# Seven block products in the last hidden group of the second block's MLP

## The chip, the cores and the metric

One NeuronCore of one Trainium2 chip runs the whole program. The metric is the device time in microseconds (us) of one execution; lower is better. A kernel's time is the median of its runs.

## The reference

Two transformer blocks work one after the other on 512 tokens of width 1024, all in float32. The change touches only the end of the second one, its MLP (y = hidden states, w1 is 1024 x 4096, w2 is 4096 x 1024):

```python
def _sq_relu_mlp(h, w1, w2):
    return jnp.square(jax.nn.relu(h @ w1)) @ w2

        y_x = _sq_relu_mlp(_modulate(x, g_pre_mlp[l], sh2, sc2), w_mlp_in[l], w_mlp_out[l])
        x = x + gt2 * _rmsnorm(y_x, g_post_mlp[l])
```

So: project up, square the ReLU, project down, normalise each token's 1024 values, scale by a gated gain, and add the residual.

## The kernel before

**Numbers.** Each float32 operand is split in a high part (rounded by ScalarE, L147) and a low part (the rest, by VectorE, L148), and a product is three matmuls: high by high, high by low, low by high (`mm3`, L150 to L154). All matmuls named below have a 128x128 stationary and a 128x512 moving operand.

**The MLP** (`mlp_seven`, called from `dense_two`, L1276). The 4096 hidden features are 32 tiles `j` of 128, in 4 groups of 8. For each group, `up(j)` makes eight tiles of the hidden activations (8 x 24 matmuls), and then the group is multiplied with its 1024 rows of w2 and added to the output.

**Groups 0 to 2** do the second part, `down(g)`, with seven block products in place of eight (Strassen's method in Winograd's form). Tokens and features are cut in two halves each. `operands` (L1298) builds four sums and differences of the quarter blocks of the hidden activations in a scratch tile (part of `gg`) and splits them; `less` (L1363) makes differences of the blocks of w2 on POOL, in place; `times` (L1343) multiplies one pair of blocks: two token tiles `tau`, two feature pairs `q`, two `i`, three matmuls, that is 24. The weights of a product are two tiles (`m2w<group><product><q>`), each loaded by one DMA of 512 KB in a ring of 6 buffers (`rb`), and split in a ring of 5 (`wh`, `wl`). Each product has two PSUM banks; its result goes to its own accumulator `Y[n]` in SBUF, by ScalarE in group 0 and by an add of VectorE afterwards (L1355, L1357).

**Then** `join()` (L1384) adds the seven accumulators up on POOL to four joined blocks, the quarters of the output: 14 adds of 128x512. The blocks are Y[2], Y[3] (token tiles 0 and 1, left and right half of the columns) and Y[4], Y[6] (token tiles 2 and 3).

**Group 3**, the last, is plain: `up` splits the activations as they are (L1330), and `token_major` (L790) multiplies them in two halves of 512 columns. A half is four token tiles x 8 `k` x 3 matmuls, so group 3 has 192 matmuls. In half 0 all four token tiles advance together, weight tile by weight tile; in half 1 (`in_turn`) one token tile is finished after the other. `evac` (L1412) adds the PSUM bank to the joined block (L1414), squares it with ScalarE for the norm (L1232), multiplies by the gain (L1416), and in half 1 POOL ends the norm (L1236, L1237), VectorE adds the residual (`post`, L1244, two halves) and SP stores it (L1419).

**Order.** The framework's scheduler lays the instructions of every engine out in one fixed order when the kernel is built: it takes what its own model of the times says is ready, the earliest in the program first. An engine then works strictly in that order, and a tile's buffer is handed on when its last reader is done. SP issues all weight loads, in order too.

Of the kernel before, what the change touches and what calls it, by code (L numbers as in the profile page):

```python
# [8 lines left out]
F32 = mybir.dt.float32  # L9
F32R = mybir.dt.float32r  # L10
# [99 lines left out]
RATIO = 1.6  # L110
TURN = "vavp"
# [18 lines left out]
class Build:  # L130
# [94 lines left out]
    def mod_T(self, x, cols_, quads, t, name, r=None):  # L225

        nc = self.nc
        xr = self.ep.tile([P, D], F32, tag="xr", name=name + "x", bufs=2)
# [5 lines left out]
        for qd in range(2):  # L234
            pt = self.turned(xr, qd, name)
            v = self.ep.tile([P, 4, P], F32, tag="v", name=f"{name}v{qd}", bufs=2)
# [991 lines left out]
    def squares(self, src, ss, half, name, tag="sqr"):  # L1228
# [3 lines left out]
        nc.scalar.activation(out=j, in_=src, func=AF.Square, accum_out=ss[:, half:half + 1])  # L1232
        if half == 0:
            nc.gpsimd.tensor_scalar(out=ss[:, 0:1], in0=ss[:, 0:1], scalar1=1.0 / D, scalar2=EPS, op0=ALU.mult, op1=ALU.add)
            return None
# [11 lines left out]
    def dense_two(self):  # L1247
# [26 lines left out]
        with ExitStack() as ph:  # L1274
            self.ep = ph.enter_context(tc.tile_pool(name="ep3", bufs=2, reuse_waits="tile"))
            self.mlp_seven(hT, a["w_mlp_in_2"][0], a["w_mlp_out_2"][0], y, gg, "m2")  # L1276

    def mlp_seven(self, hT, w1, w2, y, gg, name):

        nc = self.nc
        ac = nc.scalar.activation
        tt = nc.vector.tensor_tensor
        pt = nc.gpsimd.tensor_tensor
        ep = self.ep
        G = 8
        NG = NJ // G
        quads = [self.quad(f"{name}hid{i}").rearrange("p a b c -> p (a b c)") for i in range(2)]
        hid = quads + [ep.tile([P, 3584], F32R, tag=f"hid{i}", name=f"{name}hid{i + 2}", bufs=1) for i in range(2)]  # L1290
        more = ep.tile([P, 4, 512], F32, tag="more", name=name + "more", bufs=1)
        Y = {q: [y[i][:, h * 512:h * 512 + 512] for h in range(2)] for i, q in enumerate((2, 3, 4, 6))}
        Y[1] = [more[:, 0], more[:, 1]]
        Y[5] = [more[:, 2], more[:, 3]]
        Y[7] = [gg[:, 1, h * 512:h * 512 + 512] for h in range(2)]
        sums = gg[:, 0, :].rearrange("p (o t) -> p o t", o=4)

        def operands(g, p, st):  # L1298

            a11, a21, a12, a22 = st[:, 0, 0:256], st[:, 0, 256:512], st[:, 1, 0:256], st[:, 1, 256:512]  # L1300
            tt(out=sums[:, 0], in0=a21, in1=a22, op=ALU.add)
            tt(out=sums[:, 2], in0=a11, in1=a21, op=ALU.subtract)
            tt(out=sums[:, 1], in0=sums[:, 0], in1=a11, op=ALU.subtract)
            tt(out=sums[:, 3], in0=a12, in1=sums[:, 1], op=ALU.subtract)
            hi, lo = parts_of(p)
            self.split(hi[:, 3:7], lo[:, 3:7], sums)
            self.split(hi[:, 1:3].rearrange("p o t -> p (o t)"), lo[:, 1:3].rearrange("p o t -> p (o t)"), st[:, 1])

        def parts_of(p):
            return [hid[p][:, x * 1792:(x + 1) * 1792].rearrange("p (o t) -> p o t", o=7) for x in range(2)]  # L1310

        def plain(j):

            return hid[j % G // 2][:, j % 2 * 1024:j % 2 * 1024 + 1024].rearrange("p (x t) -> p x t", x=2)

        def up(j, st):
            wh, wl = self.weights(f"{name}u{j}", [(0, self.kview(w1, 0, KC, j * P, P))], KC, P, eng=nc.gpsimd if j < WPJ else None)
            acc = self.ps("s", f"{name}up{j}")
            nsp = 2 if j < NSP else 1
            w = SEQ // nsp  # L1320
            for sp in range(nsp):
                cols = slice(sp * w, (sp + 1) * w)
                for k in range(KC):
                    hqd = hT[k // 4]
                    self.mm3(acc[:, cols], wh[:, k, :], wl[:, k, :], hqd[:, k % 4, 0, cols], hqd[:, k % 4, 1, cols], k == 0, k == KC - 1)
            s = st[:, j % 2]
            ac(out=s, in_=acc, func=AF.Relu)
            nc.vector.scalar_tensor_tensor(out=s, in0=acc, scalar=0.0, in1=s, op0=ALU.max, op1=ALU.mult)  # L1328
            if j // G == NG - 1:
                self.split(plain(j)[:, 0], plain(j)[:, 1], s)  # L1330
            elif j % 2 == 0:
                hi, lo = parts_of(j % G // 2)
                self.split(hi[:, 0], lo[:, 0], s[:, 0:256])

        def block(g, q, r, c):

            t = ep.tile([P, 1024], F32, tag="rb", name=f"{name}d{g}{q}{r}{c}", bufs=6).rearrange("p (a b) -> p a b", a=2)
            j = g * G + 4 * q
            src = w2[j * P:(j + 4) * P, c * 512:c * 512 + 512].rearrange("(i r p) e -> r p i e", r=2, p=P)[r]
            nc.sync.dma_start(out=t, in_=src)  # L1340
            return t

        def times(g, n, o, b):  # L1343

# [14 lines left out]
        def down(g):  # L1359
            def blocks(r, c):  # L1360
                return [block(g, q, r, c) for q in range(2)]
# [89 lines left out]
```

## Time and profile before

| | us |
|---|---|
| median of 3 runs | 1255.91 (1252.36 to 1256.43) |
| the profiled execution, its own time | 1260.07 |
| its span, first to last instruction | 1258.3 |
| PE busy | 1213.5 (96%) |
| DVE busy | 844.6 (67%) |
| POOL busy | 355.1 (28%) |

PE is TensorE's matmuls, PEld its weight loads, DVE VectorE, ACT ScalarE, POOL GpSimd, SP SyncE (which issues DMAs). The span is 1.8 us shorter than the execution's own time. [...] A matmul's own duration (about 0.39 us) is longer than the distance from one start to the next, since they overlap; so costs of matmuls are taken from a stretch divided by their count.

### The profile page before, as it was taken

Reading aid. Unit: us, or ns where it says so; the run is one execution under the profiler, and the core shown is the slowest. Engines: PE = TensorE matmul, PEld = TensorE weight load, DVE = VectorE, ACT = ScalarE, POOL = GpSimd, SP = SyncE. Lnnn points to the kernel's source line nnn. Section 1 sums busy time; section 2 is a strip of 40 time slices with the busy share of each in tenths; the row PEclk is TensorE's granted clock in tenths of the full one; section 3 lists DMA queues with packets and bytes.
Section 4 is the critical chain, followed back from the end, with each engine's and each line's share of the span. In section 5 each row is a group of like instructions: output and inputs, shape, how many; then the busy total and the mean of one; then the engine's idle time right before and its main releaser. Section 6 shows DMA issues by size and latency. Waiting matters only on the chain. (4 is left out here: it accounts for less than half of the span.)

```text
span 1258.3 us, 16992 instructions
## 1 busy us (share of the span) xinstructions
PE 1213.5 (96%) x6316; PEld 1017.5 (81%) x6316; DVE 844.6 (67%) x1410; ACT 567.3 (45%) x1068; POOL 355.1 (28%) x370
## 2 busy tenths in 40 slices
PE   7899999999999999999999999999899999999997
PEld 6898888779888878888889878777798888888885
DVE  3799766597898854346355557574868678777744
ACT  5576656434223313225254546463546454343431
POOL 2787552252010000000014124030642504205502
PEclk9899999999999999999999999999999999999999
DMA  6222222365678734134145311215443643524421
GB/s 165 64 60 53 57 63 68 101 183 154 197 220 258 240 119 138 67 101 135 67 151 157 84 53 52 85 38 201 124 162 102 185 123 117 147 81 134 150 68 67
DMA packets 151707, 150.71 MB, mean 120 GB/s; under 512 B 14345, under 2 KB 115480, under 8 KB 151624
## 3 DMA queue, kind: packets, MB, share of 16 engines
q1 hardware_dynamic: 147224, 139.41, 36.4%
q0 software_dynamic: 4400, 10.22, 2.6%
q8 instruction: 49, 0.80, 0.3%
q14 instruction: 34, 0.28, 0.1%
HBM read 143.24 MB, written 6.36 MB: 119 GB/s over the span
## 5 line engine op out<-in xcount | busy, mean ns | idle before, releaser
L1365 POOL TENSOR_TENSOR m2d<-m2d,m2d 128x1024 f32<-128x1024 f32 x24 | 71.2, 2981 | 162.2 <-DVE m2w220l L148 51.5
L898 DVE SCALAR_TENSOR_TENSOR macc<-mod,silu_c,macc 128x1024 f32<-128x1024 f32 x56 | 76.1, 1369 | 15.5 <-DMA mod<-in_w_mod_dram 15.2
L975 DVE SCALAR_TENSOR_TENSOR xa<-m1d,r,xa 128x512 f32<-128x512 f32 x32 | 23.8, 746 | 37.5 <-PE m1d L154 37.5
L918 POOL DMA_DIRECT2D modrows<-mrow x8 | 3.9, 492 | 146.4 <-DVE mrow L916 91.9
L147 ACT ACTIVATE m2hid<-m2sq 128x512 fp32r<-128x512 f32 (+1 forms) x32 | 17.6, 551 | 49.1 <-DVE m2sq L1328 49.1
L147 ACT ACTIVATE m1hid<-m1sq 128x512 fp32r<-128x512 f32 x32 | 20.0, 630 | 38.3 <-DVE m1sq L844 38.3
L148 DVE TENSOR_TENSOR npl<-t,nph 128x512 fp32r<-128x512 f32 x32 | 21.7, 682 | 16.4 <-ACT nph L147 16.3
L194 POOL TENSOR_SCALAR p<-p,d 128x512 f32<-128x512 f32 x8 | 14.0, 1752 | 57.1 <-DVE d L1116 27.3
L148 DVE TENSOR_TENSOR m2hid<-m2sq,m2hid 128x512 fp32r<-128x512 f32 (+1 forms) x32 | 24.3, 760 | 6.0 <-ACT m2hid L147 5.8
L181 POOL TENSOR_SCALAR w<-w,g_attn 128x384 f32<-128x384 f32 x20 | 25.8, 1297 | 9.1 <-DMA w<-in_w_in_dram 6.7
L148 DVE TENSOR_TENSOR m1hid<-m1sq,m1hid 128x512 fp32r<-128x512 f32 x32 | 22.0, 687 | 9.1 <-ACT m1hid L147 9.1
L683 DVE TENSOR_REDUCE mb<-sb 128x1 f32<-128x128 f32 (+3 forms) x32 | 15.6, 487 | 16.5 <-PE sb L680 16.4
L1115 ACT ACTIVATE p<-s,m 128x512 f32<-128x512 f32 x32 | 22.0, 688 | 5.8 <-DVE m L1113 5.8
L1069 POOL TENSOR_TENSOR tb<-G,nam 128x256 f32<-128x256 f32 x24 | 17.8, 774 | 22.1 <-DVE m L1109 12.5
L685 ACT ACTIVATE pb<-sb,mb 128x128 f32<-128x128 f32 (+3 forms) x32 | 16.8, 525 | 16.0 <-DVE mb L683 15.7
L843 ACT ACTIVATE m1re<-m1up 128x512 f32<-128x512 f32 x32 | 18.6, 583 | 10.1 <-PE m1up L154 9.8
L204 POOL TENSOR_SCALAR nc_0ss<-nc_0ss 128x1 f32<-128x1 f32 x1 | 0.2, 187 | 80.5 <-ACT nc_0x L256 80.5
L152 PE MATMUL pj<-w_0h,xnT 128*128 128x384 f32 (+1 forms) x48 | 18.0, 376 | 4.9 <-ACT pjs L407 3.9
L147 ACT ACTIVATE nph<-t 128x512 fp32r<-128x512 f32 x32 | 19.0, 595 | 7.5 <-PE t L1126 7.2
L981 POOL DMA_DIRECT2D xspill<-xa x4 | 2.6, 655 | 70.0 <-DVE xa L975 69.9
L844 DVE SCALAR_TENSOR_TENSOR m1sq<-m1up,m1re 128x512 f32<-128x512 f32 x32 | 21.8, 683 | 0.1
L1328 DVE SCALAR_TENSOR_TENSOR m2sq<-m2up,m2sq 128x512 f32<-128x512 f32 x32 | 21.9, 684 | 0.0
(2017 smaller groups left out, 4679.7 us busy)
## 6 DMA issues: line engine op xcount, KB each, us to landing
mod<-in_w_mod_dram SPq DMA_DIRECT2D x48, 512.0 KB, 4.6
m2d<-in_w_mlp_out_dram SPq DMA_DIRECT2D x44, 512.0 KB, 3.7
m1u<-in_w_up_dram SPq DMA_DIRECT2D x32, 512.0 KB, 4.3
m1d<-in_w_down_dram SPq DMA_DIRECT2D x32, 512.0 KB, 3.6
m2u<-in_w_mlp_in_dram SPq DMA_DIRECT2D x32, 512.0 KB, 4.1
w<-in_w_in_dram SPq DMA_DIRECT2D x16, 512.0 KB, 4.2
w<-in_w_in_dram SPq DMA_DIRECT2D x48, 128.0 KB, 2.6
o1w<-in_w_out_dram SPq DMA_DIRECT2D x8, 512.0 KB, 3.8
```

Of the source, the lines that this page charges most:

```text
L147: self.nc.scalar.activation(out=hi, in_=src, func=AF.Copy)
L148: (eng or self.nc.vector).tensor_tensor(out=lo, in0=src, in1=hi.bitcast(F32), op=ALU.subtract)
L152: mm(out=out, lhsT=lh, rhs=rh, start=start, stop=False)
L181: eng.tensor_scalar(out=rv[:, i], in0=rv[:, i], scalar1=g, scalar2=None, op0=ALU.mult)
L843: ac(out=r, in_=acc, func=AF.Relu)
L844: nc.vector.scalar_tensor_tensor(out=s, in0=acc, scalar=0.0, in1=r, op0=ALU.max, op1=ALU.mult)
L898: nc.vector.scalar_tensor_tensor(out=accs[s], in0=rw, scalar=sc[:, s, k:k + 1], in1=accs[s], op0=ALU.mult, op1=ALU.add)
L975: nc.vector.scalar_tensor_tensor(out=x[t][:, cols], in0=acc, scalar=r2[:, t:t + 1], in1=x[t][:, cols], op0=ALU.mult, op1=ALU.add)
L1069: nc.gpsimd.tensor_tensor(out=tb[:, h, y], in0=G[:, h, ::-1, o:o + 32][:, :, ::-1], in1=nam[:, y, :].unsqueeze(1).to_broadcast([P, 8, 32]) ...
L1115: ac(out=pr, in_=s, func=AF.Exp, bias=m[:, 2:3], accum_out=den[:, 0:1])
L1328: nc.vector.scalar_tensor_tensor(out=s, in0=acc, scalar=0.0, in1=s, op0=ALU.max, op1=ALU.mult)
L1365: pt(out=o, in0=x, in1=z, op=ALU.subtract)
```

## The change

Group 3 takes seven block products too. For this the accumulators are arranged otherwise: product 1 goes to two of them, Y[6] and Y[2], in every group, so six accumulators do (`into`), and `joined` has ten POOL adds in place of fourteen. It leaves the four joined blocks in Y[2], Y[3], Y[4], Y[5]. `last_seven` runs products 1, 5, 6, 7, 4, 3, 2 on group 3, and adds each straight to the joined blocks that it belongs to, some of it on POOL. The last product, number 2, is done one token tile after the other (`in_turn`). Its two blocks of w2 are loaded a second time, since the first copy has been overwritten by `less`. The operands are now built in place in the activation tile, after the split of its raw second half.

The core of the diff (the removed code is in the listing above; `last_plain` is added but not called, `mod_T` gets an unused argument, `block`, `parts_of` and `less` are as before):

```diff
+        def up(j, seven):
...
+            hi, lo = parts_of(j % G // 2)
+            if j % 2 == 0:
+                self.split(hi[:, 0], lo[:, 0], s[:, 0:256])
+                return
+            self.split(hi[:, 1:3].rearrange("p o t -> p (o t)"), lo[:, 1:3].rearrange("p o t -> p (o t)"), s)
+            a11, a21, a12, a22 = st[:, 0, 0:256], st[:, 0, 256:512], st[:, 1, 0:256], st[:, 1, 256:512]
+            tt(out=a22, in0=a21, in1=a22, op=ALU.add)
+            tt(out=a21, in0=a11, in1=a21, op=ALU.subtract)
+            tt(out=a11, in0=a22, in1=a11, op=ALU.subtract)
+            tt(out=a12, in0=a12, in1=a11, op=ALU.subtract)
+            self.split(hi[:, 3:7], lo[:, 3:7], st.rearrange("p f (x t) -> p (f x) t", x=2))
...
+        def times(g, n, o, b, evac, in_turn=False):
+
+            accs = [self.ps("a", f"{name}p{g}{n}{tau}") for tau in range(2)]
+            w = [self.parts(f"{name}w{g}{n}{q}", b[q], 2, 512) for q in range(2)]
+            for q, tau in ([(0, 0), (1, 0), (0, 1), (1, 1)] if in_turn else [(0, 0), (0, 1), (1, 0), (1, 1)]):
...
+                if in_turn and q == 1:
+                    evac(tau, accs[tau])
+            if not in_turn:
+                for tau in range(2):
+                    evac(tau, accs[tau])
+
+        def down(g):
+            def into(*ns):
+                def evac(tau, acc):
+                    for n, first in ns:
+                        if g == 0 and first:
+                            ac(out=Y[n][tau], in_=acc, func=AF.Copy)
+                        else:
+                            tt(out=Y[n][tau], in0=acc, in1=Y[n][tau], op=ALU.add)
...
+            times(g, 1, 0, b11, into((6, True), (2, True)))
...
+        def joined():
+
+            for out, p, q, op in ((7, 6, 7, ALU.add), (4, 7, 4, ALU.subtract), (3, 3, 5, ALU.add), (3, 6, 3, ALU.add), (5, 7, 5, ALU.add)):
+                for tau in range(2):
+                    pt(out=Y[out][tau], in0=Y[p][tau], in1=Y[q][tau], op=op)
...
+        def last_seven(done, fetch_x):
+
+            g = NG - 1
+            f = [ep.tile([P, 2, 512], F32, tag="st", name=f"{name}f{i}", bufs=2) for i in range(2)]
+            u, c = Y[6], Y[7]
+            p1, p5 = [[x[:, 0], x[:, 1]] for x in f]
+
+            def evac1(tau, acc):
+                ac(out=p1[tau], in_=acc, func=AF.Copy)
+                pt(out=Y[2][tau], in0=Y[2][tau], in1=p1[tau], op=ALU.add)
+
+            def evac5(tau, acc):
+                ac(out=p5[tau], in_=acc, func=AF.Copy)
+                for n in (3, 5):
+                    pt(out=Y[n][tau], in0=Y[n][tau], in1=p5[tau], op=ALU.add)
+
+            def evac6(tau, acc):
+                tt(out=u[tau], in0=acc, in1=p1[tau], op=ALU.add)
+                pt(out=Y[3][tau], in0=Y[3][tau], in1=u[tau], op=ALU.add)
+
+            def evac7(tau, acc):
+                tt(out=c[tau], in0=acc, in1=u[tau], op=ALU.add)
+                tt(out=Y[5][tau], in0=Y[5][tau], in1=c[tau], op=ALU.add)
+                done(2 + tau, 1, True, Y[5][tau])
+                pt(out=Y[4][tau], in0=Y[4][tau], in1=c[tau], op=ALU.add)
+
+            def evac4(tau, acc):
+                tt(out=Y[4][tau], in0=Y[4][tau], in1=acc, op=ALU.subtract)
+                done(2 + tau, 0, False, Y[4][tau])
+
+            def evac3(tau, acc):
+                tt(out=Y[3][tau], in0=acc, in1=Y[3][tau], op=ALU.add)
+                done(tau, 1, True, Y[3][tau])
+
+            def evac2(tau, acc):
+                tt(out=Y[2][tau], in0=acc, in1=Y[2][tau], op=ALU.add)
+                done(tau, 0, False, Y[2][tau])
+            b11 = blocks(g, 0, 0)
+            times(g, 1, 0, b11, evac1)
+            t1 = blocks(g, 0, 1)
+            less(t1, t1, b11)
+            times(g, 5, S1, t1, evac5)
+            t2 = blocks(g, 1, 1)
+            less(t2, t2, t1)
+            times(g, 6, S2, t2, evac6)
+            b21 = blocks(g, 1, 0)
+            less(b21, t2, b21)
+            b22 = blocks(g, 1, 1)
+            b12 = blocks(g, 0, 1)
+            less(b12, b22, b12)
+            times(g, 7, S3, b12, evac7)
+            fetch_x((2, 3))
+            times(g, 4, A22, b21, evac4)
+            times(g, 3, S4, b22, evac3)
+            fetch_x((0, 1))
+            times(g, 2, A12, blocks(g, 1, 0), evac2, True)
...
+            self.row(gg[:, 1, :], 5)
...
+            def done(t, half, first, z):
+                r = self.squares(z, ss2[t], 0 if first else 1, f"sk{half}{t}", "sqr")
+                nc.vector.tensor_tensor(out=z, in0=z, in1=gg[:, 1, half * 512:half * 512 + 512], op=ALU.mult)
+                if not first:
+                    for _, c in self.post(x[t], [Y[((2, 3), (4, 5))[t // 2][i]][t % 2] for i in range(2)], r):
+                        nc.sync.dma_start(out=self.out[0, t * P:(t + 1) * P, c], in_=x[t][:, c])
```

## Rows read from the trace of the kernel before

**Rows 1.** The page's first lines: span, and PE's busy time.

```profile
span 1258.3 us, 16992 instructions
PE 1213.5 (96%) x6316; PEld 1017.5 (81%) x6316; DVE 844.6 (67%) x1410; ACT 567.3 (45%) x1068; POOL 355.1 (28%) x370
```

**Rows 2.** Windows: group 1's down part, group 3's up part and products, the tail.

```profile
core 0: us, PE busy (x) PEld busy (x) DVE busy (x) ACT busy (x) POOL busy (x), PEclk, DMA share, GB/s
...
1038.04:1076.84 38.80, 38.80 (x169) 31.62 (x168) 35.37 (x29) 14.59 (x15) 21.14 (x8) 1.00 0.40 131
...
1160.44:1205.23 44.79, 44.79 (x193) 36.05 (x192) 28.68 (x26) 18.18 (x25) 16.60 (x11) 1.00 0.43 135
1205.23:1249.50 44.27, 44.27 (x193) 35.92 (x191) 19.58 (x26) 10.29 (x20) 5.66 (x10) 1.00 0.15 54
1249.50:1258.30 8.80, 0.23 (x1) 0.00 (x0) 2.80 (x4) 0.72 (x2) 1.30 (x2) 0.81 0.24 92
```

**Rows 3.** Windows of one tile's instructions: `m2p` (group 0's products), `m2d` (group 3's).

```profile
954.43:993.24 38.81, 38.81 (x168) 31.44 (x167) 0.00 (x0) 6.54 (x12) 1.00 0.41 128
...
1205.23:1249.50 44.27, 44.27 (x192) 35.92 (x191) 9.54 (x11) 4.22 (x4) 0.00 (x0) 1.00 0.15 54
```

**Rows 4.** Timeline of DVE after group 1's last up: start, duration, what.

```profile
1039.16 1.23 DVE L148 TENSOR_TENSOR m2w160l<-m2d,m2w160h 128x1024 fp32r<-128x1024 f32 x1 [1.65 <-ACT m2w160h L147]
...
1042.18 1.23 DVE L148 TENSOR_TENSOR m2w161l<-m2d,m2w161h 128x1024 fp32r<-128x1024 f32 x1 [0.28 <-ACT m2w161h L147]
...
1044.26 0.68 DVE L148 TENSOR_TENSOR m2hid<-m2sq,m2hid 128x512 fp32r<-128x512 f32 x1
...
1046.59 1.22 DVE L148 TENSOR_TENSOR m2hid<-g_post,m2hid 128x1024 fp32r<-128x1024 f32 x1
1048.01 3.14 DVE L148 TENSOR_TENSOR m2w121l<-m2d,m2w121h 128x1024 fp32r<-128x1024 f32 x1 [0.20 <-ACT m2w121h L147]
```

**Rows 5.** Timeline of PE: its return to product 5 in group 1.

```profile
1050.33 0.39 PE L152 MATMUL m2p<-m2w151h,m2hid 128*128 128x512 f32 x1
```

**Rows 6.** Timeline of all engines around product 7's weights in group 2.

```profile
1143.11 2.40 POOL L1365 TENSOR_TENSOR m2d<-m2d,m2d 128x1024 f32<-128x1024 f32 x1 [5.82 <-DVE m2w230l L148]
...
1145.48 2.27 POOL L1389 TENSOR_TENSOR y<-m2more,y 128x512 f32<-128x512 f32 x1
...
1147.71 3.39 POOL L1365 TENSOR_TENSOR m2d<-m2d,m2d 128x1024 f32<-128x1024 f32 x1
...
1151.07 1.29 POOL L1389 TENSOR_TENSOR y<-m2more,y 128x512 f32<-128x512 f32 x1
1151.13 1.06 ACT L147 ACTIVATE m2w271h<-m2d 128x1024 fp32r<-128x1024 f32 x1 [4.52 <-POOL m2d L1365]
```

**Rows 7.** DMA issues: the blocks of w2; KB each, us to landing.

```profile
m2d<-in_w_mlp_out_dram SPq DMA_DIRECT2D x44, 512.0 KB, 3.7
```

**Rows 8.** Groups of DVE from 1205.23 us on: count, busy us, mean ns, idle before.

```profile
L1244 DVE SCALAR_TENSOR_TENSOR xc<-y,ss,xc 128x512 f32<-128x512 f32 x8 | 5.7, 749 | 3.2 <-POOL ss L1237 3.2
L1416 DVE TENSOR_TENSOR y<-y,g_post 128x512 f32<-128x512 f32 x8 | 5.5, 690 | 4.0 <-ACT sk L1232 3.6 <-issue 0.3
L1414 DVE TENSOR_TENSOR y<-m2d,y 128x512 f32<-128x512 f32 x8 | 5.4, 687 | 6.1 <-PE m2d L154 6.1
```

**Rows 9.** Timeline of the tail, from the last matmul on.

```profile
1249.34 0.39 PE L154 MATMUL m2d<-m2d13h,m2hid 128*128 128x512 f32 x1
1249.76 0.69 DVE L1414 TENSOR_TENSOR y<-m2d,y 128x512 f32<-128x512 f32 x1 [1.10 <-PE m2d L154]
1250.55 0.63 ACT L1232 ACTIVATE sk<-y 128x512 f32<-128x512 f32 x1 [4.83 <-DVE y L1414]
...
1251.37 0.75 POOL L1236 TENSOR_SCALAR ss<-ss 128x1 f32<-128x1 f32 x1 [4.16 <-ACT sk L1232]
1252.21 0.55 POOL L1237 TENSOR_TENSOR ss<-ss,nhalf 128x1 f32<-128x1 f32 x1
1252.79 1.42 DVE L1244 SCALAR_TENSOR_TENSOR xc<-y,ss,xc 128x512 f32<-128x512 f32 x2 [0.80 <-POOL ss L1237]
```

More of the change, by code (lines that the diff above doesn't have):

```diff
@@ L110 @@
 RATIO = 1.6
+MRAW = 4
+RB_2 = 6
 TURN = "vavp"
@@ L223, in split_T, with mod_T @@
             self.split(quads[qd][:, :, 0, cols], quads[qd][:, :, 1, cols], self.turned(x, qd, name))
-    def mod_T(self, x, cols_, quads, t, name, r=None):
+    def mod_T(self, x, cols_, quads, t, name, r=None, tiles=None):
         nc = self.nc
-        xr = self.ep.tile([P, D], F32, tag="xr", name=name + "x", bufs=2)
+        xr, vtag = tiles or (self.ep.tile([P, D], F32, tag="xr", name=name + "x", bufs=2), "v")
         if r is None:
@@ L235, in mod_T @@
             pt = self.turned(xr, qd, name)
-            v = self.ep.tile([P, 4, P], F32, tag="v", name=f"{name}v{qd}", bufs=2)
+            v = self.ep.tile([P, 4, P], F32, tag=vtag, name=f"{name}v{qd}", bufs=2 if vtag == "v" else MRAW)
             for j in range(4):
@@ L1230, in squares @@
+    def squares(self, src, ss, second, name, tag="sqr"):
         nc = self.nc
         j = self.ep.tile([P, 512], F32, tag=tag, name=name, bufs=2)
-        nc.scalar.activation(out=j, in_=src, func=AF.Square, accum_out=ss[:, half:half + 1])
-        if half == 0:
+        nc.scalar.activation(out=j, in_=src, func=AF.Square, accum_out=ss[:, second:second + 1])
+        if not second:
             nc.gpsimd.tensor_scalar(out=ss[:, 0:1], in0=ss[:, 0:1], scalar1=1.0 / D, scalar2=EPS, op0=ALU.mult, op1=ALU.add)
@@ new lines, in dense_two @@
+            hidx = self.ep.tile([P, 7168], F32R, tag="hidx", name="m2hidx", bufs=1)
+            more = self.ep.tile([P, D], F32, tag="more", name="m2more", bufs=1)
+            Y = {n: [b[:, h * 512:h * 512 + 512] for h in range(2)]
+                 for n, b in ((2, y[0]), (3, y[1]), (4, y[2]), (5, y[3]), (6, more), (7, gg[:, 0, :]))}
+            self.row(gg[:, 1, :], 5)
+            last_ups, last_plain, last_seven = self.mlp_seven(hT, a["w_mlp_in_2"][0], a["w_mlp_out_2"][0], hidx, Y, RB_2, lambda: None, "m2")
@@ new lines, in dense_two, with fetch_x @@
+            x = {}
+            ss2 = [self.small("ss", f"ss2{t}") for t in range(NT)]
+            def fetch_x(ts):
+                for t in ts:
+                    x[t] = self.ep.tile([P, D], F32, tag="rb", name=f"xc{t}", bufs=RB_2)
+                    nc.sync.dma_start(out=x[t], in_=self.xspill2[t * P:(t + 1) * P, :])
+            def done(t, half, first, z):
[3 more added lines that the diff above has]
+                    for _, c in self.post(x[t], [Y[((2, 3), (4, 5))[t // 2][i]][t % 2] for i in range(2)], r):
@@ L1419, in evac @@
                         nc.sync.dma_start(out=self.out[0, t * P:(t + 1) * P, c], in_=x[t][:, c])
-            j = (NG - 1) * G
-            self.token_major(f"{name}d{half}", G,
-                             lambda q: self.weights(f"{name}d{half}{q}", [(0, self.kview(w2, j + 2 * q, 2, half * 512, 512))], 2, 512),
-                             lambda i: plain(j + i), evac, half == 1)
+            last_ups(True, lambda j: None)
+            last_seven(done, fetch_x)
 _INS = ['x', 'attn_norm_g', 'w_in', 'b_forget', 'q_norm_a', 'k_norm_a', 'sink_logits', 'q_norm_b', 'k_norm_b', 'w_out',
```

216 lines of the change are left out of this document (91 added, 125 removed).

## The prediction

> **What bounds the kernel now.** I read the page first, then the stretches of the second MLP, then single engines in the last of them. PE is busy for 96% of the span [rows 1], which alone says little, because matmuls overlap. The stretches say more [rows 2]: in a down part (group 1), in group 3's up part and in group 3's products PE is busy for the whole of each (38.80 of 38.80, 44.79 of 44.79, 44.27 of 44.27 us) at a granted clock of 1.00. No wait of PE is left to remove there; only fewer matmuls shorten it. The other engines have room, DVE least: 35.37 of 38.80 us in a down part with POOL at 21.14, but 19.58 of 44.27 in group 3's products, where POOL does 5.66. So the change takes work from the full engine and gives some to the two that have room in just that stretch.
>
> The kernel ends with a chain of dependent small steps after the last matmul, 8.80 us [rows 2, 9].
>
> **What is removed.** Group 3's plain products are 2 halves x 4 token tiles x 8 k x 3 = 192 matmuls, in 44.27 us, 0.2306 each. A group of seven products is 7 x 24 = 168, in 38.80 us, 0.2310 each [rows 3]. The difference is 24 matmuls: 44.27 - 38.80 = 5.5 us off PE. Up parts and groups 0 to 2 keep their matmul counts.
>
> **What is added, engine by engine.** Let P be the end of the last up, 1205.23 us, where product 1 of group 3 will start. A product lasts 38.80 / 7 = 5.54 us, so the order 1, 5, 6, 7, 4, 3, 2 puts product 7 at P + 16.6, product 2 at P + 33.3, and the end of PE at P + 38.8.
>
> DVE between P and the end: ten weight tiles to split (products 6, 7, 4, 3, 2; those of 1 and 5 are done during the ups) x 1.22 = 12.2 [rows 4]; twelve adds from PSUM x 0.69 = 8.2, eight multiplies by the gain x 0.69 = 5.5, eight residual steps x 0.75 = 6.0 [rows 8]; and the last pair's operands, two ops of 0.68, one of 1.22 and four smaller ones, say 4. That is 35.9, of which 2.8 lie in the tail as before [rows 9]: 33 us in 38.8. It fits, if POOL lets it.
>
> POOL: ten adds (two, four, two and two for products 1, 5, 6, 7) x 1.29 and two `less` for product 7 x 2.40 = 17.7 us when undisturbed [rows 6], 29.5 at the disturbed 2.27 and 3.39. It fits as well. The other six `less` of the group come before P, `joined` is shorter than `join` by four adds, and both lie under the ups.
>
> ACT gets four copies of PSUM (0.63 each, as its square of the same size [rows 9]) and the ten splits at 1.06 [rows 6]: 13 us beside the eight squares. No cost. SP issues 14 block loads in place of eight weight loads, which are spread over the stage at 3.7 us to landing [rows 7]; the x tiles now come later, behind product 7's and 4's splits, and are wanted only after product 4, 11 us on. No cost. The early gain row on POOL's queue is one DMA issue in a stage that is not changed. No cost. Product 1's second accumulator adds two DVE adds of 0.69 per group: 1.4 us in a down part where DVE has 38.80 - 35.37 = 3.4 us left [rows 2]. No cost while that is left.
>
> **Three places where it can leak.**
>
> First, the operands. The raw second half is now split before the in-place sums, which puts one ACT step of 0.6 and one DVE step of 0.68 ahead of the last split, and two more DVE adds come near it. In group 1 that split ended at 1047.81 [rows 4], and PE came back to the matmuls that use it at 1050.33 [rows 5]: 2.5 us spare. 1.3 + 1.4 = 2.7 uses them up. If the split slides past 1048, POOL's `less` meets it, and it takes 3.14 in place of 1.22 [rows 4]. Bounds: nothing, if the scheduler fills in other matmuls as it did there, to 2 us in each of four groups, 8 in all. I take 0.2 per group, near the lower end, since the spare time about equals the delay and PE had no gap in these stretches: 0.8.
>
> Second, product 7's weights. Their blocks reuse the buffers of product 6's, which in group 1 were split 2.4 and 5.4 us after the last up ended at 1038.0 [rows 4]. So: P + 2.4 and P + 5.4, plus 3.7 to landing [rows 7] gives P + 6.1 and P + 9.1; `less` at up to 3.39, one after the other, ends at P + 9.5 and P + 12.9 at the latest; split by ACT and DVE (2.3, up to 4.2 disturbed) ends at P + 12 to 14 and P + 15 to 17. PE wants them at P + 16.6 and P + 19.4. Two to four us spare. Bounds: nothing to 10 (second rival). I take nothing: the forecast has POOL do these `less` as soon as they are ready, and it has done so out of the program's order before: an add of `join` (L1389) ran between two `less` of the group before it [rows 6].
>
> Third, the tail. The last token tile follows the one before by 12 matmuls, 2.8 us; in the kernel before it was 24, 5.5 us. The residual step of the first one comes 1252.79 - 1249.73 = 3.06 us after its last matmul [rows 9], so it wants DVE 0.3 us after the last tile's add does. If the fixed order has it first, the add waits 0.3 + 1.42 = 1.7 us; otherwise it waits for nothing. Bounds 0 and 1.7; I take 0.4, as the add is ready first.
>
> **The sum.** -5.5 + 0.8 + 0 + 0.4 = -4.3 us. It stands against the profiled execution, 1260.1 us (span 1258.3): 1255.8. The median of the runs shown is 4.2 lower, 1255.9, and I carry that difference over: **1251.6 us**. Its own bounds: with nothing lost 1250.4, with 2 us more lost 1253.6.
>
> **Rivals.** About 0.3% (3.8 us) is what a measurement of this kernel can tell from no change; below 1252.1 counts as faster.
>
> *DVE becomes the second bound, and the gain goes into its waits.* A split beside a POOL op took 3.14 in place of 1.22, 1.9 more [rows 4], and ten splits and twelve POOL ops now share 38.8 us. If half the splits meet one, DVE needs 33 + 5 x 1.9 = 42.5 us, 3.7 too many. Against it: in group 2 the second tile of product 7 waited 4.52 us for POOL and was split at 1151.13 + 1.06 + 1.22 = 1153.4 [rows 6], while PE wanted it at 1160.44 - 2.8 = 1157.7: 4.3 us of lead even so. For it: product 2's blocks are loaded late, into buffers that product 3's splits set free, so a late DVE delays that load too. Price: about 2.5 us more than the forecast, 1254.1. Chance 0.29.
>
> What POOL costs DVE could also follow a stricter rule. The row shows an op of 1.22 us stretched to 3.14 beside one of POOL's [rows 4]. If every POOL op held DVE up for its whole length, 33 + 17.7 = 50.7 us would be wanted of 38.8, and the kernel would be 11.9 - 5.5 + 0.4 = 6.8 us slower, 1262.7. [...] Chance 0.03.
>
> *POOL's order starves product 7 (slower).* POOL works strictly in its built order. In the program the adds of products 1 and 5 stand ahead of the `less` for product 7. If the scheduler leaves the second `less` behind them, it starts when product 5's four adds are done: they begin at P + 11.1 + 0.6, last 4 x 2.27, and end at P + 20.8; then 3.39 for the `less`, 1.06 and up to 3.14 for the split: P + 28.4, against P + 19.4 wanted. PE idles 9 us, and the rest follows it: -5.5 + 9 + 1.2 = +4.7, 1260.6. With both `less` behind them it is 3.4 more. It decides once product 7's second split ends later than P + 28, 9.3 us after PE wants it. For it: the two adds of product 1 alone use up the spare time. Against it: [rows 6], as above. Chance 0.10.
>
> *It doesn't do what it says.* The scheduler lays out the whole program anew, and other tiles share the space; the earlier stages could shift by a few us either way. Nothing in their program changes. Chance 0.02, 1256.
>
> **How the numbers follow.** The forecast has 0.56, the first rival 0.29, the lock 0.03, POOL's order 0.10, the last 0.02. Most of the forecast's bounds lie below 1252.1; I count 0.54 of it and 0.03 of the first rival as faster: 0.57. Within 0.3%: 0.02 + 0.26 + 0.03 of cases that end between 1252.1 and 1259.7 = 0.31. Slower: 0.12. The range reaches from 1249.7 (nothing lost, and under a microsecond for the median itself) to 1256.5, which takes in nearly all of the first rival and leaves the slower ones out.
>
> **What would show it.** Right: 168 matmuls `m2p` of group 3 in 38.8 to 39.5 us with PE busy throughout; POOL's two last `less` before product 5's adds; a tail of 8.8 to 9.3 us. First rival: gaps in PE ahead of products 4, 3 or 2, ended by DVE splits of 2 to 3 us. Second: one gap of 9 us ahead of product 7, ended by ACT or DVE after POOL. Wrong altogether: a stretch before 1121 us that changed its length, or a gap in the ups.

## The result, and the profile after

The changed kernel takes **1263.27 us** (median of 6 runs, 1260.38 to 1265.91); the kernel before, beside it, 1256.57 (6 runs, 1252.36 to 1259.27). The ratio is 1.0054 [1.0033, 1.0075]: **slower**, by 6.7 us, where 4.3 less was forecast. The profiled execution took 1265.91 us. Line numbers from here on are those of the kernel at hand, some lines off those of before.

The page's first lines of the kernel after, which answer to [rows 1]:

```profile
span 1264.1 us, 17044 instructions
PE 1208.5 (96%) x6292; PEld 1009.8 (80%) x6292; DVE 888.1 (70%) x1448; ACT 577.8 (46%) x1080; POOL 387.6 (31%) x384
```

The matmuls did go: 24 fewer, and PE is busy 5 us less. DVE is busy 43.5 us more and POOL 32.5 more. The windows of group 1's down part, group 3's ups, its products, and the tail, which answer to [rows 2] (PEclk there is the clock granted to TensorE as a share of its full one; the products end here 0.23 us, a matmul's distance, behind the start of the last matmul):

```profile
1036.92:1077.25 40.33, 39.42 (x169) 31.44 (x168) 35.14 (x33) 14.47 (x15) 17.30 (x7) 1.00 0.39 118
...
1162.37:1207.54 45.17, 44.95 (x193) 36.04 (x192) 36.66 (x39) 18.71 (x25) 25.82 (x14) 1.00 0.36 104
1207.54:1249.06 41.52, 39.67 (x169) 31.16 (x167) 39.40 (x37) 18.32 (x27) 28.62 (x18) 1.00 0.40 127
1249.06:1264.10 15.04, 0.16 (x1) 0.00 (x0) 8.98 (x14) 2.89 (x8) 4.01 (x6) 0.64 0.27 106
```

Before, PE was busy for the whole of each of the first three. Now it has gaps in all of them, and the tail, in which PE does nothing, is 15.0 us for 8.7. DVE works 39.4 of 41.5 us in the products and goes on for 9 us behind them.

Ahead of group 0's down part the change touches only group 0's operands and the gain row. That stretch differs by several us between the profiles: the down part starts between 946.0 (experiment 9) and 954.7 us (experiment 2). So kernels are compared by their stages from there on, each counted from first matmul to first matmul:

```
                    down 0  down 1  down 2  ups 3  products  tail   sum (with ups 1, 2: 44.79 each, all)
before               38.81   38.81   38.81  44.79     44.33   8.73  303.9
after                39.00   40.34   40.32  45.18     41.52  15.06  311.0
```

By stages the change costs 7.1 us: -2.8 in the products (-5.5 were due), +6.3 in the tail, +3.2 in the down parts, +0.4 in the ups. The table goes on at the experiments.

**The down parts.** Timeline of DVE in group 1's down part of after (start, duration, line, what), then of POOL in the same stretch, then PE's return to the last pair of product 5; they answer to [rows 4, 5]:

```profile
1046.67 3.42 DVE L150 TENSOR_TENSOR m2w121l<-m2d,m2w121h 128x1024 fp32r<-128x1024 f32 x1
1050.02 0.41 DVE L1280 TENSOR_TENSOR m2sq<-m2sq 128x256 f32<-128x256 f32 x1
1050.46 2.52 DVE L1281 TENSOR_TENSOR m2sq<-m2sq 128x256 f32<-128x256 f32 x1
...
1054.56 1.22 DVE L150 TENSOR_TENSOR m2hidx<-m2sq,m2hidx 128x1024 fp32r<-128x1024 f32 x1
```

```profile
1046.55 2.46 POOL L1298 TENSOR_TENSOR m2d<-m2d,m2d 128x1024 f32<-128x1024 f32 x1 [50.08 <-DVE m2w120l L150]
1050.23 2.47 POOL L1298 TENSOR_TENSOR m2d<-m2d,m2d 128x1024 f32<-128x1024 f32 x1 [1.21 <-issue]
```

```profile
1054.58 0.50 PE L154 MATMUL m2p<-m2w151h,m2hidx 128*128 128x512 f32 x1 [0.81 <-ACT m2hidx L149]
```

The operands' last split starts 17.6 us after the last up (1036.9), where it started 8.6 us after it before. It slid behind two of POOL's `less`: the sum of 0.42 us that meets the second takes 2.52. PE runs out of other matmuls and waits.

**The products and the tail.** Timeline of DVE from product 5's result on, then the POOL row beside it:

```profile
1226.15 2.32 DVE L150 TENSOR_TENSOR m2w340l<-m2d,m2w340h 128x1024 fp32r<-128x1024 f32 x1
1228.40 1.27 DVE L1376 TENSOR_TENSOR m2more<-m2p,m2f 128x512 f32<-128x512 f32 x2
1229.60 1.21 DVE L150 TENSOR_TENSOR m2w341l<-m2d,m2w341h 128x1024 fp32r<-128x1024 f32 x1
1230.73 2.32 DVE L150 TENSOR_TENSOR m2w330l<-m2d,m2w330h 128x1024 fp32r<-128x1024 f32 x1
1232.97 0.68 DVE L1380 TENSOR_TENSOR g_post<-m2p,m2more 128x512 f32<-128x512 f32 x1
...
1238.61 1.78 DVE L1381 TENSOR_TENSOR y<-y,g_post 128x512 f32<-128x512 f32 x1
...
1249.48 0.68 DVE L1390 TENSOR_TENSOR y<-m2p,y 128x512 f32<-128x512 f32 x1
...
1255.02 0.68 DVE L1394 TENSOR_TENSOR y<-m2p,y 128x512 f32<-128x512 f32 x1
```

```profile
1225.48 8.72 POOL L1373 TENSOR_TENSOR y<-y,m2f 128x512 f32<-128x512 f32 x4 [2.60 <-ACT m2f L1371]
```

Four adds of 1.29 us alone take 8.72 beside DVE, 2.18 each. Of the three splits shown beside them two take 2.32 for 1.22, and the one at 1229.60 keeps 1.21. The adds from PSUM (L1376, L1380) keep their 0.68. The last two rows of DVE show the lateness that comes of it: product 3 ends where product 2's first matmul starts, at 1242.14, and its first add runs at 1249.48. DVE is 7 us behind PE, and the tail is the time in which it catches up.

PE's own 2.7 us of gaps in the products lie at two places, about half at each: at the return to the last pair of product 5, which waits for the operands' splits, and inside product 2, where a weight split comes late. The longest of each:

```profile
1224.02 0.50 PE L156 MATMUL m2p<-m2w351h,m2hidx 128*128 128x512 f32 x1 [0.60 <-DVE m2hidx L150]
...
1245.01 0.50 PE L155 MATMUL m2p<-m2w321l,m2hidx 128*128 128x512 f32 x1 [1.07 <-DVE m2w321l L150]
```

### The profile page after: what moved, and what is told of

The parts are those of the page before. It is cut to its first block, busy times and chain, and to the rows that moved or that the text cites. A ratio compares the mean times of both kernels' runs of the same rounds, so it can differ in the third digit from the quotient of the medians.

```text
span 1264.1 us, 17044 instructions
## 1 busy us (share of the span) xinstructions
PE 1208.5 (96%) x6292; PEld 1009.8 (80%) x6292; DVE 888.1 (70%) x1448; ACT 577.8 (46%) x1080; POOL 387.6 (31%) x384
## 3 DMA queue, kind: packets, MB, share of 16 engines
q1 hardware_dynamic: 148856, 142.55, 37.1%
## 5 line engine op out<-in xcount | busy, mean ns | idle before, releaser
L1298 POOL TENSOR_TENSOR m2d<-m2d,m2d 128x1024 f32<-128x1024 f32 x32 | 88.7, 2783 | 188.6 <-DVE m2w220l L150 50.3
L149 ACT ACTIVATE m2hidx<-m2sq 128x256 fp32r<-128x256 f32 (+2 forms) x24 | 16.7, 701 | 29.1 <-DVE m2sq L1269 14.9
L149 ACT ACTIVATE m2hid<-m2sq 128x256 fp32r<-128x256 f32 (+2 forms) x24 | 16.9, 703 | 28.7 <-DVE m2sq L1269 22.1
L150 DVE TENSOR_TENSOR m2hid<-m2sq,m2hid 128x256 fp32r<-128x256 f32 (+2 forms) x24 | 23.6, 1000 | 5.6 <-ACT m2hid L149 5.6
L150 DVE TENSOR_TENSOR m2hidx<-m2sq,m2hidx 128x256 fp32r<-128x256 f32 (+2 forms) x24 | 21.0, 884 | 4.0 <-ACT m2hidx L149 3.9
```

The costliest lines, as they stand in the source:

```text
L149: self.nc.scalar.activation(out=hi, in_=src, func=AF.Copy)
L150: (eng or self.nc.vector).tensor_tensor(out=lo, in0=src, in1=hi.bitcast(F32), op=ALU.subtract)
L1298: pt(out=o, in0=x, in1=z, op=ALU.subtract)
```

## The experiments

The kernel before ran beside each set on the same chip, with medians of 1256.6 us (first four), 1256.84 (next three), 1258.08 (next four) and 1256.97 (last). Stages of each profile, in us, as above:

```
                    down 0  down 1  down 2  ups 3  products  tail   sum   ratio to before
e1_scratch           39.61   38.84   38.84  44.79     45.11  15.75  312.5  1.0059 [1.0041, 1.0077]
e2_no_pool_adds      39.03   40.32   40.32  45.17     38.87  11.19  304.5  1.0019 [1.0004, 1.0034]
e3_no_turn           38.92   40.32   40.32  45.37     40.56  14.49  309.6  1.0045 [1.0027, 1.0062]
e4_no_gain           38.94   40.30   40.32  46.43     40.24  13.11  308.9  1.0039 [1.0025, 1.0052]
e5_scratch_no_adds   39.70   38.83   38.84  44.79     40.58  13.52  305.8  1.0012 [0.9998, 1.0026]
e6_no_joined         38.92   40.33   40.32  44.79     41.51  15.07  310.5  1.0065 [1.0043, 1.0088]
e7_late_join         39.68   38.84   38.83  44.79     38.81  16.46  307.0  1.0019 [1.0003, 1.0034]
e8_adds_unread       39.00   40.32   40.32  46.45     39.66  14.50  309.8  1.0017 [1.0001, 1.0034]
e9_adds_on_dve       39.01   40.33   40.32  44.79     39.19  11.66  304.9  1.0017 [0.9999, 1.0034]
e10_add_first        39.03   40.33   40.33  46.43     41.47  15.07  312.2  1.0051 [1.0035, 1.0068]
e11_scratch_early    39.16   38.84   38.84  44.79     41.41  15.05  307.7  1.0023 [1.0009, 1.0037]
e12_both_mended      39.09   38.83   38.84  44.79     39.15  11.71  302.0  0.9984 [0.9969, 1.0000]
```

A sum is that of one profiled execution; a ratio is of all runs, and its interval is about 2 us wide either way. The sum's distance from before (303.9) lies inside that interval for every run but experiment 8.

**1. The operands in a spare tile, as before** (and so the gain row, whose space that tile takes, after the ups):

```diff
-            self.split(hi[:, 1:3]..., s)
-            tt(out=a22, in0=a21, in1=a22, op=ALU.add)
...
+            tt(out=sums[:, 3], in0=a21, in1=a22, op=ALU.add)
...
+            self.split(hi[:, 3:7], lo[:, 3:7], sums)
+            self.split(hi[:, 1:3]..., s)
```

> The changed kernel with its operands built as in the kernel before: the four sums go to a scratch tile ahead of the split of the raw second half (the scratch is the second half of the gain tile, so the gain row is loaded after the ups). Theory A (the in-place operands are what makes the last pair of a group late): the down parts of groups 1 and 2 go from 40.33 us back to 38.8 us each, PE has no gap in them, and the time falls by about 3 us; group 3's products start 3 us earlier and, since the last pair's operands leave VectorE sooner, the stretch from their start to the end falls too, from 56.6 us by 1 to 4 us. Theory B (POOL's adds next to VectorE are the cause of everything): the down parts, which have only the weight differences on POOL as before, stay at 40.3 us or change by less than 0.5 us.

1263.7 us. Downs 1 and 2 are back at 38.84, with PE never idle. But products and tail went from 56.6 to 60.9, and the time stayed. That the operands' new place and order (the edit undoes both together) cause the gaps in the downs is shown. What they cost is not won by this edit: the operands are built in the same way in group 3, and products and tail lose 4.3 us there. Experiment 11 takes the two apart.

**2. Without the ten POOL adds of group 3's products:**

```diff
-                pt(out=Y[2][tau], in0=Y[2][tau], in1=p1[tau], op=ALU.add)
...
-                pt(out=Y[4][tau], in0=Y[4][tau], in1=c[tau], op=ALU.add)
```

> The changed kernel without the ten adds that POOL makes in group 3's products (products 1, 5, 6 and 7 are then missing in parts of the output; all matmuls, splits and VectorE's steps stay). Theory B (VectorE is late because POOL's adds hold up its steps that read two operands from SBUF): VectorE's busy time from the start of group 3's products to the end falls from 48.4 us to about 38 us, the products take 39 to 40 us in place of 41.8, the tail falls from 14.8 us to 9 to 10 us, and the time falls by 6 to 8 us. Theory C (VectorE has too many steps there even without POOL): the busy time falls by less than 4 us, the tail stays above 12 us and the time falls by under 3 us. Under both the down parts of groups 1 and 2 stay at 40.3 us.

1259.19 us. The windows of its products and tail:

```profile
1209.09:1247.96 38.87, 38.87 (x169) 31.40 (x167) 34.84 (x43) 19.67 (x33) 9.16 (x10) 1.00 0.44 149
1247.96:1259.10 11.14, 0.16 (x1) 0.00 (x0) 4.67 (x7) 0.72 (x2) 2.53 (x4) 0.67 0.25 94
```

PE is busy throughout, and products and tail take 6.5 us less than after (50.06 for 56.58). DVE's busy time falls from 39.40 + 8.98 = 48.4 to 39.5, though none of its own instructions was taken away: ten adds on POOL cost DVE 8.9 us. By the ratios the gain is 4.4 us (1.0019 for 1.0054), less than the 6 to 8 expected. The tail is still 2.5 above before.

**3. The last product with both token tiles together:**

```diff
-            times(g, 2, A12, blocks(g, 1, 0), evac2, True)
+            times(g, 2, A12, blocks(g, 1, 0), evac2)
```

> The changed kernel with its last product done as the others, both token tiles together, so that both results are ready at the very end. Theory D (the tail is long because the last token tile follows the one before by only 2.8 us, the third leak of the prediction): both now follow at once, and the tail grows by 2 us or more. Theories B and C (VectorE is behind by several us by then, so that PE's end doesn't matter): tail and time change by less than 1.5 us.

1261.72 us; products and tail 55.05, 1.5 less than after. Taking the token tiles in turn, then, doesn't save time here. A likely reason, not tested, is that DVE is so late that a token tile finished early only sets more small steps ahead of the last one.

**4. Without the eight gain multiplies:**

```diff
-                nc.vector.tensor_tensor(out=z, in0=z, in1=gg[:, 1, half * 512:half * 512 + 512], op=ALU.mult)
```

> The changed kernel without VectorE's eight multiplies by the gain in group 3 (the output then lacks the gain of the post-MLP norm). They are 8 x 0.69 = 5.5 us of VectorE's work, up to 1.8 us each beside POOL, in its last third. Theory C (too many steps of VectorE): the time falls by 4 to 7 us, all of it in the products and the tail. Theory B: the time falls by about the multiplies that lie after VectorE has fallen behind, 3 to 5 us, and POOL's adds keep the rest. The two differ more in e2; what this run tells is whether any microsecond of VectorE in that stretch is a microsecond of the kernel.

1260.2 us; products and tail 53.35, 3.2 less, for 8 x 0.69 = 5.5 us of DVE. So DVE's time counts here, but not one for one. (The ups of group 3 took 46.43 in this profile, 1.3 more; experiment 10 shows that this need not be the edit's.)

**5. Experiments 1 and 2 together:**

> Both edits of the first two runs at once: operands through the scratch tile, and no POOL adds in group 3's products (parts of the output are then missing). If the in-place operands and POOL's adds are the two causes and nothing else is, the down parts are 38.8 us, group 3's products 38.8 us without a gap of PE, the tail 9 to 10 us, and the time lies 4 to 5 us below the kernel before. If VectorE is behind already when group 3's products start, because of the ten adds of the joining beside group 3's ups (the new theory E: in the changed kernel the last two ReLU squares of the ups come 7 and 5 us after their matmuls), the products stay 1 us or more above 38.8 us or the tail above 10.5 us, and the time is at best 2 to 3 us below the kernel before.

1258.78 us. The two don't add up: the spare tile gives 3.0 in downs 1 and 2, and takes 4.0 in products and tail (54.1 for 50.06). That loss is group 3's own: without POOL's adds it is still there.

**6. Without `joined`'s ten POOL adds beneath the ups:**

```diff
-            joined()
             for j in range((NG - 1) * G, NJ):
```

> The changed kernel without the ten POOL adds of the joining, which lie beside group 3's ups (the output is then wrong in three of the four blocks). Theory E (they make VectorE late before the products start, and the lateness is carried to the tail): group 3's ups go from 45.17 us back to 44.8 us, the last ReLU squares follow their matmuls within 3 us, and the stretch from the first of group 3's products to the end falls from 56.6 us by 2 to 4 us. If VectorE's lateness at the end is made by what happens in the products alone (POOL's adds there), that stretch stays within 1 us of 56.6 us, although the ups are clean.

1264.51 us. The ups are 0.4 shorter, and DVE's last square starts 2.5 us after the start of its last matmul, where it was 5.0. Yet products and tail are the same to 0.01 us (56.58). That DVE starts the products late was my own next suspicion, and it falls.

**7. No joining ahead; instead running sums, six POOL adds for twenty, order 1, 5, 2, 6, 3, 7, 4; spare tile:**

```diff
-            joined()
...
+            times(g, 1, 0, b11, add(2, 6))
...
+            times(g, 5, S1, t1, add(5, then=((3, 5),)))
...
+            times(g, 6, S2, t2, add(6, then=((3, 6), (7, 6))))
...
+            times(g, 4, A22, b21, evac4, True)
```

> A version that computes all. Operands through the scratch tile; the blocks aren't joined ahead of group 3 at all: group 3's products 1, 5, 6 and 7 are added to their accumulators from PSUM by VectorE as in the groups before, and the joining is done once, as the accumulators become final, six adds on POOL and four on VectorE, in place of ten on POOL beside the ups and ten more beside the products. The products come in the order 1, 5, 2, 6, 3, 7, 4, so that token tiles 0 and 1 are finished two products before the end. VectorE has six more steps of 0.69 us, POOL 14 adds fewer. If POOL's adds are what stretches VectorE's steps, the down parts are 38.8 us, group 3's ups 44.8 us, its products 39 to 40 us and the tail 9 to 11 us: 2 to 4 us faster than the kernel before. If VectorE's own count of steps is what matters, the six more cost 4 us, and it is no faster than the kernel before.

1259.47 us. PE is busy for the whole of the products:

```profile
1204.94:1243.75 38.81, 38.81 (x169) 31.41 (x167) 32.46 (x34) 14.99 (x21) 24.48 (x17) 1.00 0.29 97
1243.75:1260.20 16.45, 0.16 (x1) 0.00 (x0) 11.47 (x19) 2.89 (x8) 4.52 (x6) 0.58 0.33 128
```

All of the 5.5 us is there, and the tail takes 7.7 back, with 11.5 us of DVE in it. DVE idles 6 us in the products: 3.0 at its adds that wait for POOL's, 2.5 at a split that waits for ACT. A full PE alone tells nothing of the end. (The run also gives the products more PSUM banks, so it doesn't single out one cause.)

**8. The ten POOL adds stay, but nobody reads them:**

```diff
+            spare = ep.tile([P, 496], F32, tag="spare", name="spare", bufs=1)
...
-                pt(out=Y[2][tau], in0=Y[2][tau], in1=p1[tau], op=ALU.add)
+                pt(out=spare, in0=p1[tau][:, 0:496], in1=p1[tau][:, 0:496], op=ALU.add)
```

> Leaves a part out: the ten adds of group 3 on POOL are there, at the same places, but each adds the product's copy (or sum) to itself into a spare tile that nothing reads (496 columns of 512), so no instruction waits for any of them and the joined blocks lack those terms. It splits what leaving the adds out gave back (2.65 us in the products and 3.87 in the tail: 41.52 + 15.06 became 38.87 + 11.19). Theory 'beside': POOL's adds lengthen DVE's instructions that run beside them, waited for or not: products and tail stay within 1 us of 56.6 together, 1262.5 to 1264. Rival 'waits': DVE's instructions stand in a fixed order behind ones that wait for POOL's results: with nobody waiting, products and tail go to 50 to 51 together, 1258 to 1259.5. In between, both have a share, in proportion.

1260.79 us, products and tail 54.16: between the two theories. Of the 6.5 us that leaving the adds out gives in the profiles, 4.1 are lost with nobody waiting. The other 2.4 need not be waits, since the adds are also shorter: with one tile as both inputs, and 496 columns of 512, the shortest take 1.01 us, for 1.29. The profile of after names what DVE waited for from the products on (us in total, times, longest), 3.8 us in all, and none of it is one of the ten adds:

```profile
DVE xc L1450 <- POOL ss L1443: 1.6, 3, 0.7
DVE m2hidx L150 <- ACT m2hidx L149: 1.1, 1, 1.1
DVE y L1498 <- ACT sk L1438: 1.1, 2, 0.8
```

So the profiles put the loss down to DVE running beside POOL. The measured times don't confirm this run's share of it: its ratio, 1.0017, can't be told from the 1.0019 of experiment 2, which has no adds at all, and its profile's sum, 5.9 us over before, lies outside the ratio's interval (0.1 to 4.3 us).

**9. The ten adds on DVE:**

```diff
-                pt(out=Y[2][tau], in0=Y[2][tau], in1=p1[tau], op=ALU.add)
+                tt(out=Y[2][tau], in0=Y[2][tau], in1=p1[tau], op=ALU.add)
```

> Complete: the ten adds of group 3 run on DVE in place of POOL, 10 x 0.69 = 6.9 us of DVE more, and POOL's 12.9 us gone. If an add on POOL costs DVE as much as it takes from the kernel (6.5 us over ten, 0.65 each), then an add on DVE is no dearer, and the time is that of after, 1262 to 1264.5. If DVE had slack that POOL's adds don't use (DVE is busy for 37.1 of 38.9 us in the products without the adds), up to 2 us of the 6.9 are free: 1261 to 1262. Rival: DVE is not the bound at all and only waits for POOL matter: 1258 to 1259.5.

1260.57 us, 3.7 thousandths under after by the ratios, which is 4.7 us. Products and tail are 50.85: the ten adds cost 0.8 us on DVE, 6.5 on POOL, by the profiles; by the ratios nothing (1.0017 beside 1.0019) and 4.4. The theory, that they cost as much on either, falls. The windows of products and tail, and DVE's row of splits and adds:

```profile
1200.08:1239.27 39.19, 39.15 (x169) 31.33 (x167) 38.69 (x49) 18.62 (x31) 10.97 (x10) 1.00 0.40 128
1239.27:1250.90 11.63, 0.16 (x1) 0.00 (x0) 6.86 (x11) 1.45 (x4) 3.15 (x4) 0.64 0.41 158
```

```profile
1223.79 1.21 DVE L150 TENSOR_TENSOR m2w330l<-m2d,m2w330h 128x1024 fp32r<-128x1024 f32 x1
1224.92 0.68 DVE L1377 TENSOR_TENSOR y<-y,m2more 128x512 f32<-128x512 f32 x1
1225.52 1.22 DVE L150 TENSOR_TENSOR m2w331l<-m2d,m2w331h 128x1024 fp32r<-128x1024 f32 x1
...
1227.26 0.68 DVE L1381 TENSOR_TENSOR y<-y,g_post 128x512 f32<-128x512 f32 x1
...
1234.94 0.68 DVE L1390 TENSOR_TENSOR y<-m2p,y 128x512 f32<-128x512 f32 x1
```

DVE is busy 38.69 + 6.86 = 45.55 us, 6.0 more than without the adds, 0.60 each; on POOL they took 0.89 each from DVE. (The 37.1 us of the expectation adds up durations that overlap a little; the window has 34.84.) The rest of the gain is idle time: behind DVE's last instruction the store takes 4.05 us in after and here, so of 56.56 us DVE idled 56.56 - 48.38 - 4.05 = 4.1 before its end, and here 50.82 - 45.55 - 4.05 = 1.2. Product 3's add at 1234.94 is 1.2 us behind PE, not 7.

**10. The first token tile's residual steps written behind the last add:**

```diff
-                done(tau, 0, False, Y[2][tau])
+                rest.append(done(tau, 0, False, Y[2][tau]))
+                if tau == 1:
+                    for r in rest:
+                        r()
```

> Complete: only the order of the text in the last product: the two residual steps of the first token tile are written behind the second token tile's add from PSUM, not ahead of it. In the profile without POOL's adds the last add started at 1250.64, 2.5 us after PE's last matmul, behind two residual steps that waited for POOL; that is all of what its tail (11.19) has over that of before (8.73). In the profile of after the last add started at 1255.02, its tile being ready near 1249.3. Theory 'order': 2 to 2.5 us less, 1261 us. Rival 'DVE is late anyway': in after DVE is behind by more than those steps take, and moving 1.5 us of work behind the add puts it onto the end again: 0 to 0.8 us less, 1262.5 to 1263.3.

1265.04 us, tail 15.07. This tested nothing: the profile shows DVE's order unchanged, because the scheduler had the last add ahead of those steps in after already (in the profile of experiment 2 it had not). In after it stands behind a gain multiply that waits for ACT's square. The run is of use as a repeat: PE, DVE, ACT and POOL run the same instructions in the same order as in after, from the down parts on. Products and tail come out the same to 0.04 us (56.54 and 56.58), while the ups of group 3 take 46.43 for 45.18. So differences of 1.3 us in the ups need no other kernel.

**11. The spare tile in groups 0 to 2 alone:**

```diff
+            if j < (NG - 1) * G:
+                tt(out=sums[:, 3], in0=a21, in1=a22, op=ALU.add)
...
+                return
```

> Complete: the operand sums go to a spare tile, with their split ahead of the raw halves' split, in groups 0 to 2 alone; group 3 keeps the sums in place, and the gain row is loaded before its ups. In all four groups this gave downs 1 and 2 their 1.5 us each back (38.84 each) and lost as much in group 3. Theory: those 3.0 us come back and group 3 stays as in after: 1260.3 us, u3 45.2, products 41.5, tail 15.1. Rival: with PE 3 us earlier the same lateness of DVE shows in group 3 all the same, because DVE's work and not PE's sets the end there: 1262.5 to 1263.5.

1261.01 us, ratio 1.0023. Downs 1 and 2 are at 38.84, and products and tail (56.46) stay as in after: the theory's numbers. The rival falls: the 3 us of the downs are a loss of their own.

**12. Experiments 9 and 11 together:**

> Complete: the operand sums in a spare tile in groups 0 to 2, and group 3's ten adds on DVE in place of POOL, together. Theory: the two causes are separate and add up. Stage by stage from the profiles of the two alone, against before: down 0 39.16 for 38.81, downs 1 and 2 38.84 for 38.81 each, group 3's ups 44.79 for 44.79, its products 39.19 for 44.33, tail 11.66 for 8.73: 0.35 + 0.06 - 5.14 + 2.93 = -1.8 us against before, 0.9986 of its time, and 3.3 below the adds on DVE alone and 5.3 below the spare tile alone by stages. Rival: DVE holds both ends of the account, and what one edit takes off downs 1 and 2 returns in the products and the tail, as it did where all four groups had the spare tile (products 45.11, tail 15.75): products and tail 53 to 55 together in place of 50.9, time 0.3% above before.

**1254.34 us** (12 runs, 1252.46 to 1259.61), ratio 0.9984 [0.9969, 1.0000]: 2.0 us under before, 1.8 expected; the interval ends at no change. The windows of group 1's down part, group 3's ups, products and tail:

```profile
1033.08:1071.92 38.84, 38.84 (x170) 31.59 (x168) 36.60 (x31) 14.47 (x15) 20.03 (x8) 1.00 0.41 128
...
1155.55:1200.34 44.79, 44.79 (x194) 36.03 (x193) 36.20 (x43) 20.21 (x27) 27.69 (x13) 1.00 0.34 102
1200.34:1239.49 39.15, 39.15 (x169) 31.32 (x167) 37.12 (x47) 18.43 (x29) 10.85 (x10) 1.00 0.40 127
1239.49:1251.20 11.71, 0.16 (x1) 0.00 (x0) 6.90 (x11) 1.45 (x4) 3.16 (x4) 0.66 0.41 157
```

PE is busy in every stretch again, and the two causes add up. By stages they take back 9.0 us (311.0 to 302.0), of 7.1 lost. The tail keeps 3.0 us over before: 11 DVE instructions lie in it, in before four. The rows of its end, which answer to [rows 9]:

```profile
1241.78 0.68 DVE L1402 TENSOR_TENSOR y<-m2p,y 128x512 f32<-128x512 f32 x1
...
1245.70 1.41 DVE L1459 SCALAR_TENSOR_TENSOR xc<-y,ss,xc 128x512 f32<-128x512 f32 x2 [0.72 <-POOL ss L1452]
```

The last add starts 2.3 us after the end of the products, for 0.2 in before, and the residual steps follow it after 3.9 us, for 3.0. That places the 3.0 us; no run tried to remove them.

## Why the prediction was wrong

- **The matmuls** (-5.5): right. Products of 38.81 to 38.87 us in experiments 2 and 7, for 44.33. It was paid out and taken back elsewhere.
- **First leak, the operands** (0.8): mechanism right, size wrong. It named the place, the 2.7 us of delay against 2.5 spare, and the meeting with POOL's `less`; then it took 0.2 per group, "near the lower end", where 0.2, 1.5 and 1.5 came in downs 0 to 2, inside its bounds. Spare time just used up isn't a small cost: once the split slid, it met not one `less` but two. In group 3 it shows too: about half of PE's 2.7 us of gaps in the products lie at the return to product 5's last pair, though they go when POOL's adds go (experiment 2).
- **Second leak, product 7's weights** (0): right. In after PE goes on to product 7's tiles at 1225.52 and 1226.90 with no gap ahead of either. The second rival (POOL's order) didn't come.
- **Third leak, the tail** (0.4, at most 1.7): failed. It was worked out for a DVE that is on time. The tail grew by 6.3, since DVE is 7 us late when PE ends.
- **"It fits, if POOL lets it"**: here the prediction failed. It had DVE at 33 us in 38.8; DVE needed 39.4 in the products, and 9.0 in the tail. Two terms were too small. What DVE still owes at the last up is one: a square, two splits of 1.22 and smaller ones, 4 us. (In experiment 6 DVE starts the products 2.5 us less late, and gains nothing, so this isn't the one that decides.) The other decides: ten adds on POOL take 8.9 us of DVE (experiment 2). The adds were costed on POOL alone, "17.7 us when undisturbed", as work that an idle engine does; their price on DVE was put at nothing in the sum.
- **The first rival**, DVE as second bound, is what happened, at chance 0.29, but not at its price, 2.5 us over the forecast, where 11 us came. The lengthening that it took, 9.5 us, is near the 8.9 of experiment 2, though it put all of it on splits. The gain multiplies, and two of the "twelve adds from PSUM" (L1381), read two tiles in SBUF and are lengthened too (1.78 for 0.68). Too small was the work under it: 35.9 us with the tail's part, where DVE needs 39.5 without POOL's adds. And the price isn't worked out from the 3.7 us that it finds too many: it leaves out that what DVE can't do while PE works comes after it. Its sign came in part: PE has no gap in products 4 and 3, and one in product 2, ended by a split of 1.21 us.
- **The stricter rule**, at 0.03, gave 1262.7 us, within a microsecond of the result. That it came so near is partly luck: it had products and tail 6.8 us over before, 3.5 were measured, and the other 3.6 came from the downs and the ups. Nor does a POOL add hold DVE up for its whole length, as it had it: 0.89 us each in experiment 2, for 1.29 alone. A price below that is there, and DVE's 35.37 us beside POOL's 21.14 with PE never idle [rows 2] don't speak against it: they already hold what POOL takes. By the shortest instruction of the same line and shape, seven of the 29 there are 11.7 us too long together, and each of the seven ran beside a `less` of POOL. The row shows a stage that could bear the loss, not a loss that isn't there.
- `joined` under the ups (nothing): no cost is shown. The ups are 0.4 us shorter without it (experiment 6), but as short with it in experiments 9 and 12.

What stays open: why the measured time of experiment 8 lies nearer to that of experiment 2 than its profile does, and how the last 3 us of the best tail could be removed.

## What to carry to other kernels

An add moved to an idle engine is free only if it takes nothing from the busy one: here an add of 128x512 took 0.6 us of VectorE's time when VectorE did it and 0.9 when GpSimd did; the rest of the gain from moving the adds to VectorE was less idle time there. VectorE's busy time, read from a stage with both engines at work, already contained what GpSimd took from it (11.7 of 35.37 us in group 1's down part of the kernel before); to see whether more fits, sum the shortest instruction of each kind, and count the rest as loss. And where the last engine to finish isn't the one that was relieved, look at what it owes when the other ends: a saving in matmuls can be paid out in full and come back in the tail (experiment 7: 5.5 us less in the products, 7.7 more in the tail).

## What was not expected of the hardware

In the profile of after, from group 0's down part on, 36 VectorE instructions took 0.28 us or more above the shortest of their kind and shape; each ran beside GpSimd and had its inputs in SBUF alone. None with an input in PSUM was above its shortest by over 0.05 us. Beside POOL's adds from 1225.48 on, splits with both inputs in SBUF took up to 2.32 us for 1.22 (the one at 1229.60 kept 1.21), and an add of two SBUF tiles up to 1.78 for 0.68; the adds with one input in PSUM kept 0.68 (1228.40, 1232.97). From group 0's down part on, the 19 VectorE adds with an input in PSUM that ran beside POOL's adds and `less` took 0.67 to 0.69 us. The trace shows the pattern; no run shows what causes it.

POOL pays as well: its ten adds, 1.29 us alone, took 1.56 to 2.21 on average per line, 19.7 us in all (L1368, L1373, L1377, L1383).
